# Attention mixers of a two-block decoder: the grouped heads are projected before the neighbourhood heads

## The chip, the cores and the metric

The kernel runs on one core of a Trainium2 chip, as one program. The time is in device microseconds (us), and the medians below are over several executions. One execution was also taken by the hardware profiler, and every row in this document comes from that one.

## What is computed

The first block has two layers. Each layer is a feed-forward net (FFN), four attention mixers side by side, a projection with `w_out`, and a second FFN. Then comes a second block with other mixers, which the change does not touch. There are 256 tokens, in two tiles of 128, and 1024 features. Cut to what matters:

```python
h = rms_norm(x, mix_norm[l])
pa, pb, pc, pd = jnp.split(h @ w_in[l], IN_SPLITS, axis=-1)
ya = neighbourhood_mixer(pa, ...)   # q, k normed per head; logits + bias table
yb = mla_mixer(pb, ...)             # "latent": two more projections, rotary
yc = diff_mixer(pc, ...)            # "differential": difference of two softmaxes
yd = gqa_mixer(pd, ...)             # "grouped": q, k normed, axial rotary, no bias
x = x + jnp.concatenate([ya, yb, yc, yd], axis=-1) @ w_out[l]
x = x + 0.5 * swiglu(rms_norm(x, ffn2_norm[l]), ...)
```

Each mixer has four heads of 64 and gives 256 columns, so that each owns two of the eight row blocks of `w_out` (128 rows each): the neighbourhood heads own blocks 0 and 1, latent 2 and 3, differential 4 and 5, grouped 6 and 7.

## The kernel before

All products run as matmuls of up to 512 columns. A large product takes three of them: operands are split into a high and a low part (`xTh`, `xTl` for the activations, `hi`, `lo` for the weights), and the sum of hi·hi, lo·hi and hi·lo is kept. Weights come from HBM in units of 512 KB into three staging buffers (`st`); ScalarE (ACT) rounds a unit to `hi`, VectorE (DVE) subtracts to get `lo`. Six split buffers lie ahead of TensorE (PE), and a unit is cut when PE is done with the unit six before it.

In each layer `mixers` records the projections as a stream that PE always has work in, and the attention as background generators (`differential`, `latent`, `neighbourhood`, `grouped`) that are resumed between the matmuls of that stream. A small clock model (class `Clock`, fixed costs per operation) says when a generator is due. After that the tile scheduler places the instructions of every engine; each engine then runs its own list strictly in order.

- Projections before the change, in the order of the code: differential q and k (512 columns), latent (416), differential v (256), latent's two small ones, neighbourhood q and k (512, `un`), neighbourhood v (256, `vn`), grouped q, k and v (512, `ug`). The list of weights at the start of `decoder` has the same order.
- One softmax is at work at a time (`att["busy"]`), in `softmax_pv`. A mixer has four jobs (differential eight), and a job covers 128 queries by 256 keys of two heads. A job makes scores into two PSUM buffers (`sps`, one for each half of the job), takes a maximum on DVE (`nm`), exponentials on ACT (`E`), transposes `E` on PE (`tps`), copies it out (`PT`), multiplies with v, and transposes back (`yt`). Then DVE writes `y`. Where the logits have no bias (latent, grouped) the exponential reads `sps` itself, so the buffer is free only after it; with a bias (neighbourhood, differential) DVE reads `sps` and frees it.
- When a mixer's jobs for a token tile are done, `post` norms them (`yn`), PE transposes `yn`, and ACT and DVE write it as `yT`, high and low.
- `neighbourhood` and `differential` keep their transposed q and k in the `xg` buffers (`qkT` in the profile); `latent` and `grouped` share one pair (`qT`, `kT`), so `grouped` waits for `"mla_s"`, latent's last scores.
- `wide` then runs the product with `w_out` over `OUT_ORDER`: four units one by one (blocks 4, 5, 2, 3; for each both token tiles and both halves of 512 columns), then the last four together, half by half. `before(k, t)` holds a matmul back until that mixer's `yT` of that token tile is recorded. The first matmuls of the FFN's gate (`xTh`, `xTl`) follow as soon as a token tile's `x` is normed.

Of the kernel before, what the change touches and what calls it, by code (L numbers as in the profile page):

```python
# [39 lines left out]
FIRST = [1, 1, 2, 2, 2]  # L40
WARM = 6
AHEAD = 14
OUT_ORDER = (4, 5, 2, 3, 0, 1, 6, 7)
IN2 = {"ax": 0, "az": 512, "bq": 1024, "bkv": 1536, "bz": 1792,
       "cq": 2304, "ck": 2816, "cv": 3328, "cz": 3840, "g": 4352}
IN2_ORDER = (("cq", 512), ("ck", 512), ("cv", 512), ("bq", 512), ("bkv", 256),
# [183 lines left out]
def decoder(ctx, tc, a, out):  # L230
# [33 lines left out]
    for l in range(L):  # L264
        for f in (1, 2):
            if f == 2:
                wi = a["w_in"][l]
                ws.add(wi, 8, 512, 2, (OFF_DIFF, OFF_DIFF + 512))
                ws.add(wi, 8, 416, 2, (OFF_MLA, OFF_MLA + 416))
                ws.add(wi, 8, 256, 4, (OFF_DIFF + 512, OFF_DIFF + 768))  # L270
                ws.add(a["mla_w_uq"][l], 2, 384, 2)
                ws.add(a["mla_w_ukv"][l], 1, 512, 1)
                ws.add(wi, 8, 512, 2, (OFF_NA, OFF_NA + 512))
                ws.add(wi, 8, 256, 4, (OFF_NA + 512, OFF_NA + 768))
                ws.add(wi, 8, 512, 2, (OFF_GQA, OFF_GQA + 512))
                for k in OUT_ORDER:
                    ws.add(a["w_out"][l][k * 128:(k + 1) * 128, :], 1, D, 1)
            for c in range(0, DFF, 512):
                n = min(512, DFF - c)
                for w in ("gate", "up"):  # L280
                    first = (l, f, c, w) == (0, 1, 0, "gate")
                    ws.add(a[f"ffn{f}_w_{w}"][l], 8, n, FIRST if first else 1024 // n,
                           (c, c + n))
            ws.add(a[f"ffn{f}_w_down"][l], KF, D, 1)
# [125 lines left out]
    def spawn(gen, first=False, at=None):  # L410
        at = clock.last if at is None else at
        bg.insert(0 if first else len(bg), [gen, at, at])
# [83 lines left out]
    def proj(K, n, per, evac, skew=False):  # L496

        ps = [psM() for _ in range(2)]
        per = per if isinstance(per, list) else [per] * (K // per)
        block = len(per) if skew else 1  # L500
        k0 = 0
        for u0 in range(0, len(per), block):
            w = [get() for _ in range(block)]
            for t in range(2):
                k = k0
                for u in range(block):
                    for j in range(per[u0 + u]):
                        acc([(ps[t][:, :n], 0, n)], xTh[:, k, tok(t)], xTl[:, k, tok(t)],
                            w[u], j, k == 0, k == K - 1)
                        if k < K - 1:  # L510
                            tick()
                        k += 1
                    if t == 1:
                        ws.end(w[u])
                if k == K:
                    done = timed(evac, t, ps[t])
                    tick()
            k0 = k
        return done
# [192 lines left out]
    def mixers(l, cols, rows, nlam, norm_out):  # L712
# [43 lines left out]
        def new_v(nh):  # L756
            return wk.tile([128, 2, nh, 64], F, tag="v", name="v", bufs=3)
# [22 lines left out]
        def ev_u(u):  # L780
            return lambda t, ps: scaled(u[:, t, :], ps, rstd[t])
# [178 lines left out]
        def neighbourhood(u, v):  # L960
            qT, kT = yield from qk_transposed(u, lambda: new_qk(0), "na_q", "na_k",
                                              64 ** -0.5, 64, lambda: "diff_s" in finished)
            yield lambda: (4, 1) in finished
            y = new_y()
            jobs = []
            for t in range(2):
                for p in range(2):
                    jobs.append(dict(
                        t=t, nk=2, bias=[bias[:, t, 4 + 2 * p + s, :] for s in range(2)],
                        qk=[(pair(qT[64 * s:64 * s + 64, :, tok(t)], p),  # L970
                             pair(kT[64 * s:64 * s + 64], p)) for s in range(2)],
                        v=[[v[:, k, 2 * p + s, 0:64] for k in range(2)] for s in range(2)],
                        y=heads(y[:, t, tok(p)])))
            yield from softmax_pv(jobs, post_rms(y, "na_beta", 0),
                                  have_v=lambda: "na_v" in finished)

        def grouped(ug):
# [51 lines left out]
                split_out(kT[:, 0, tok(t)].bitcast(R), kT[:, 2, tok(t)].bitcast(R), p3[:, 2])  # L1029
                yield 0  # L1030
            yield
            yield lambda: (2, 1) in finished
            y = new_y()
            jobs = []
            for t in range(2):
# [17 lines left out]
        proj(8, 256, 4, ev_v(vd))  # L1053
        finished.add("diff_v")
        w += [get(), get()]
        un = wk.tile([128, 2, 512], F, tag="u", name="u")
        vn = new_v(4)
        spawn(neighbourhood(un, vn), at=proj(8, 512, 2, ev_u(un)))
        proj(8, 256, 4, ev_v(vn))
        finished.add("na_v")  # L1060
        ug = []

        def ev_gqa(t, ps):
# [4 lines left out]
            scaled(ug[t], ps, rstd[t])  # L1068
        at = proj(8, 512, 2, ev_gqa)
        spawn(grouped(ug), at=at)  # L1070

        def before(k, t):
            k0 = k // 2 * 2
            return (k0, t) in finished and (k0 == 6 or (k0, 1) in finished)
        wide(OUT_ORDER, yTh, yTl, [1] * 4 + [4], lambda t, h, ps: norm_out.update(t, h, ps, 1.0),
             before)

# [364 lines left out]
```

## Time and profile before

| | us |
|---|---|
| median of 3 runs | 1328.57 (1325.44 to 1332.58) |
| the profiled execution | 1329.33 |
| its span, first to last instruction | 1327.2 |

| engine | busy us | share of the span |
|---|---|---|
| PE matmuls | 1302.8 | 98% |
| PE weight loads | 1049.7 | 79% |
| DVE | 792.8 | 60% |
| ACT | 722.8 | 54% |
| POOL | 27.6 | 2% |

A PE that is shown busy is not PE at its peak, since matmuls are pipelined and their ends are modelled: what counts is from one matmul's start to the next. The mixers of the first layer run from about 202 to 345 us, those of the second from about 728 to 870 us. The profile has a clock that the throttle grants to PE, in tenths of full speed; two levels occur, full (2.4 GHz) and half (1.2 GHz).

### The profile page before, as it was taken

The page shows a single profiled execution, that of the slowest core. Times are in us where ns is not written, and L with a number is a line of the kernel's source. Part 1 is how long each engine was busy: PE and PEld are TensorE (multiplying, and loading weights), DVE is VectorE, ACT ScalarE, POOL GpSimd, SP SyncE. Part 2 cuts the span into 40 slices and gives each one's busy share as a digit, 9 for nine tenths or more (in the row PEclk, how much of TensorE's full clock was granted, in tenths as well). Part 3 has the DMA queues.
Part 4 walks back from the last instruction along what each step waited for, and adds up shares of the span by engine and source line. Part 5 has one row for each costly group of instructions (what it writes and reads, how often), then busy time and mean ns, then how long its engine had stood idle before and what let it go on. Part 6 is the DMA issues. An engine that isn't in the chain of part 4 may idle for free.

```text
span 1327.2 us, 17825 instructions
## 1 busy us (share of the span) xinstructions
PE 1302.8 (98%) x6514; PEld 1049.7 (79%) x6514; DVE 792.8 (60%) x1615; ACT 722.8 (54%) x1223; POOL 27.6 (2%) x44
## 2 busy tenths in 40 slices
PE   9999999999999999999999999999999999999997
PEld 7788888766788888788888876678888787678886
DVE  5655449895655544755545898565554565555475
ACT  6544437865644443644434676664444467566543
POOL 0000001000000000100000000000000000000000
PEclk9999999998999999999999998999999999999999
DMA  8766657432466655666665733156655484245752
GB/s 268 224 183 185 181 165 236 125 96 64 153 191 188 191 175 175 192 189 188 177 188 145 245 112 96 49 174 184 185 182 182 149 264 141 80 142 167 206 167 80
DMA packets 109815, 221.80 MB, mean 167 GB/s; under 512 B 7456, under 2 KB 30368, under 8 KB 109728
## 3 DMA queue, kind: packets, MB, share of 16 engines
q1 hardware_dynamic: 109152, 220.04, 55.5%
q8 instruction: 51, 0.84, 0.3%
q10 hardware_dynamic: 576, 0.63, 0.1%
q14 instruction: 36, 0.29, 0.1%
HBM read 219.59 MB, written 1.05 MB: 166 GB/s over the span
## 4 chain that ended last, share of the span: by engine, by line
PE 82%; DVE 6%; DMA 6%; ACT 4%; issue 1%; POOL 0%; POOLq 0%; ACTq 0%; SPq 0%; DVEq 0%
PE mmps L333 71%; PE tps L337 6%; PE sps L333 3%; PE tps L333 3%; DVE lo L154 2%; DMA st<-in_ffn_w_gate_dram 2%; DMA st<-in_w_in_dram 2%; ACT hi L154 2%; DMA st<-in_ffn_w_up_dram 2%; ACT junk L154 1%; DVE xTl L153 1%; ACT xTh L153 0%; POOL r L154 0%; DVE x L153 0%; ACT E L153 0%
## 5 line engine op out<-in xcount | busy, mean ns | idle before, releaser
L154 DVE TENSOR_TENSOR lo<-st,hi 128x1024 fp32r<-128x1024 f32 (+2 forms) x403 | 488.0, 1214 | 400.5 <-ACT hi L154 399.6
L154 ACT ACTIVATE hi<-st 128x1024 fp32r<-128x1024 f32 (+2 forms) x403 | 421.7, 1050 | 433.6 <-PE mmps L333 353.8
L333 PE MATMUL mmps<-hi,xTh 128*128 128x512 f32 (+2 forms) x1200 | 452.5, 377 | 1.3 <-ACT xTh L153 1.0
L333 PE MATMUL mmps<-hi,xTl 128*128 128x512 f32 (+2 forms) x1200 | 446.5, 372 | 0.0
L333 PE MATMUL mmps<-lo,xTh 128*128 128x512 f32 (+2 forms) x1200 | 446.3, 372 | 0.0
L333 PEld LDWEIGHTS mmps<-hi,xTh 128*128 128x128 f32 x1200 | 226.3, 189 | 43.2 <-issue 2.6
L333 PEld LDWEIGHTS mmps<-hi,xTl 128*128 128x128 f32 x1200 | 226.3, 189 | 37.8 <-issue 0.5
L333 PEld LDWEIGHTS mmps<-lo,xTh 128*128 128x128 f32 x1200 | 226.4, 189 | 36.6 <-issue 1.0
L333 PE MATMUL mmps<-lo,hTh 128*128 128x512 f32 x352 | 140.2, 398 | 0.0
L333 PE MATMUL mmps<-hi,hTh 128*128 128x512 f32 x352 | 139.8, 397 | 0.0
L333 PE MATMUL mmps<-hi,hTl 128*128 128x512 f32 x352 | 115.6, 395 | 0.0
L333 PE MATMUL mmps<-hi,yT 128*128 128x512 f32 (+1 forms) x248 | 89.8, 420 | 0.6 <-ACT yT L153 0.6
L333 PEld LDWEIGHTS mmps<-hi,hTl 128*128 128x128 f32 x352 | 66.2, 188 | 15.6
L333 PEld LDWEIGHTS mmps<-hi,hTh 128*128 128x128 f32 x352 | 66.2, 188 | 15.4
L333 PEld LDWEIGHTS mmps<-lo,hTh 128*128 128x128 f32 x352 | 66.1, 188 | 15.3
L333 PEld LDWEIGHTS mmps<-hi,yT 128*128 128x128 f32 x248 | 46.3, 191 | 12.1 <-issue 2.0
L154 POOL TENSOR_TENSOR r<-ms,mhalf 128x1 f32<-128x1 f32 x40 | 27.4, 688 | 1294.7 <-DVE ms L154 1294.6
L333 PE MATMUL mmps<-lo,yT 128*128 128x512 f32 (+1 forms) x124 | 50.4, 406 | 0.0
L154 ACT ACTIVATE E<-E,nm 128x256 f32<-128x256 f32 (+1 forms) x80 | 38.2, 480 | 14.9 <-DVE nm L154 14.7
L153 ACT ACTIVATE fg<-mmps,r 128x512 f32<-128x512 f32 (+1 forms) x48 | 31.1, 652 | 21.7 <-PE mmps L333 21.7
L153 ACT ACTIVATE xTh<-tps,gains 128x128 fp32r<-128x128 f32 x112 | 31.7, 366 | 16.8 <-PE tps L337 16.8
L153 ACT ACTIVATE PT<-tps 128x512 f32<-128x512 f32 (+1 forms) x56 | 27.9, 502 | 22.0 <-PE tps L337 21.5
(172 smaller groups left out, 1039.3 us busy)
## 6 DMA issues: line engine op xcount, KB each, us to landing
st<-in_w_in_dram SPq DMA_DIRECT2D x90, 512.0 KB, 3.8
st<-in_ffn_w_up_dram SPq DMA_DIRECT2D x88, 512.0 KB, 4.1
st<-in_ffn_w_down_dram SPq DMA_DIRECT2D x88, 512.0 KB, 3.6
st<-in_ffn_w_gate_dram SPq DMA_DIRECT2D x87, 512.0 KB, 3.8
st<-in_w_out_dram SPq DMA_DIRECT2D x24, 512.0 KB, 3.7
st<-in_w_in_dram SPq DMA_DIRECT2D x8, 416.0 KB, 4.2
scratch<-in_t5b_dram SPq DMA_DIRECT2D x4, 512.0 KB, 4.8
scratch<-in_nab_dram SPq DMA_DIRECT2D x4, 512.0 KB, 6.8
```

Of the source, the lines that this page charges most:

```text
L153: return f(*args, **kw)
L154: return f(*args, **kw)
L333: nc.tensor.matmul(ps, lhsT=lhsT, rhs=rhs, start=start, stop=stop)
L337: nc.tensor.transpose(ps, src, ident)
```

## The change

Three things move, and no operation is added or taken away. The grouped projection (one of 512 columns: q, k and v) stands directly behind differential v. Neighbourhood v comes next, and neighbourhood q and k are the last projection, so that this mixer's generator starts last. The list of weights has the same new order. In the softmaxes the grouped mixer now waits for the differential one to be finished, `(4, 1)`, and the neighbourhood mixer for the latent one, `(2, 1)`: they have changed places. `OUT_ORDER` ends with 6, 7, 0, 1, and in `before` the neighbourhood blocks are now those whose second token tile need not be done for the first to go ahead.

```diff
-OUT_ORDER = (4, 5, 2, 3, 0, 1, 6, 7)
+OUT_ORDER = (4, 5, 2, 3, 6, 7, 0, 1)
...
                 ws.add(a["mla_w_ukv"][l], 1, 512, 1)
+                ws.add(wi, 8, 512, 2, (OFF_GQA, OFF_GQA + 512))
+                ws.add(wi, 8, 256, 4, (OFF_NA + 512, OFF_NA + 768))
                 ws.add(wi, 8, 512, 2, (OFF_NA, OFF_NA + 512))
-                ws.add(wi, 8, 256, 4, (OFF_NA + 512, OFF_NA + 768))
-                ws.add(wi, 8, 512, 2, (OFF_GQA, OFF_GQA + 512))
...
         def neighbourhood(u, v):
             qT, kT = yield from qk_transposed(u, lambda: new_qk(0), "na_q", "na_k",
                                               64 ** -0.5, 64, lambda: "diff_s" in finished)
-            yield lambda: (4, 1) in finished
+            yield lambda: (2, 1) in finished
...
                 split_out(kT[:, 0, tok(t)].bitcast(R), kT[:, 2, tok(t)].bitcast(R), p3[:, 2])
                 yield 0
             yield
-            yield lambda: (2, 1) in finished
+            yield lambda: (4, 1) in finished
...
         w += [get(), get()]
-        un = wk.tile([128, 2, 512], F, tag="u", name="u")
-        vn = new_v(4)
-        spawn(neighbourhood(un, vn), at=proj(8, 512, 2, ev_u(un)))
-        proj(8, 256, 4, ev_v(vn))
-        finished.add("na_v")
         ug = []
...
         at = proj(8, 512, 2, ev_gqa)
         spawn(grouped(ug), at=at)
+        un = wk.tile([128, 2, 512], F, tag="u", name="u")
+        vn = new_v(4)
+        proj(8, 256, 4, ev_v(vn))
+        finished.add("na_v")
+        spawn(neighbourhood(un, vn), at=proj(8, 512, 2, ev_u(un)))
 
         def before(k, t):
             k0 = k // 2 * 2
-            return (k0, t) in finished and (k0 == 6 or (k0, 1) in finished)
+            return (k0, t) in finished and (k0 == 0 or (k0, 1) in finished)
```

The lists of the engines are the same up to the projection of neighbourhood v. From there on they differ, in both layers in the same way. Three places follow.

The first is PE in the first layer, where latent's first scores (`sps<-kT,qT`) stand. `u` is the neighbourhood's q and k, `yn` the differential mixer's second token tile, and `mmps<-...,yT` the product with `w_out`. Before:

```order
L337 MATMUL tps_2763<-ident_106,u_2081 128x128 x4
L337 MATMUL tps_2789<-ident_106,u_2081 128x128 x4
L333 MATMUL sps_2798<-kT_2684,qT_2683 128x256
L333 MATMUL sps_2799<-kT_2684,qT_2683 128x256
L333 MATMUL mmps_2758<-hi_2591,yT_1716 128x512
L333 MATMUL sps_2855<-kT_2684,qT_2683 128x256
L337 MATMUL tps_2868<-ident_106,E_2800 128x128 x2
L333 MATMUL sps_2856<-kT_2684,qT_2683 128x256
L337 MATMUL tps_2868<-ident_106,E_2800 128x128 x2
L333 MATMUL sps_2930<-kT_2684,qT_2683 128x256
L333 MATMUL sps_2931<-kT_2684,qT_2683 128x256
L337 MATMUL tps_2905<-ident_106,yn_2853 128x128 x2
```

After:

```order
L333 MATMUL sps_2781<-kT_2654,qT_2653 128x256
L333 MATMUL sps_2782<-kT_2654,qT_2653 128x256
L333 MATMUL mmps_2824<-hi_2570,yT_1716 128x512
L333 MATMUL mmps_2823<-hi_2630,yT_1716 128x512
L333 MATMUL mmps_2823<-lo_2631,yT_1716 128x512
L333 MATMUL mmps_2824<-hi_2630,yT_1716 128x512
L333 MATMUL mmps_2824<-lo_2631,yT_1716 128x512
L333 MATMUL mmps_2823<-hi_2630,yT_1716 128x512
L333 MATMUL mmps_2824<-hi_2630,yT_1716 128x512
L333 MATMUL sps_2845<-kT_2654,qT_2653 128x256
L333 MATMUL sps_2846<-kT_2654,qT_2653 128x256
L333 MATMUL sps_2872<-kT_2654,qT_2653 128x256
```

The eight transposes of `u` are gone from here, seven matmuls of `w_out` stand between the first job's scores and the second's, and the scores of the second job and half of the third now stand in one piece; `yn` follows that piece.

The second is DVE between the same `y` and `yn`, its last twelve rows. Before (`hss`, `ms`, `r`, `q` are the steps of a reciprocal square root, here of the grouped heads and of `y`):

```order
L153 TENSOR_REDUCE nm<-sps 128x1
L154 SCALAR_TENSOR_TENSOR r<-q,r 128x4
L154 TENSOR_SCALAR r<-ms 128x6
L154 TENSOR_REDUCE hss<-scratch 128x6
L154 SCALAR_TENSOR_TENSOR q<-ms,r 128x4
L153 TENSOR_REDUCE nm<-sps 128x1
L154 TENSOR_TENSOR q<-q,r 128x4
L154 TENSOR_SCALAR ms<-hss 128x6
L154 SCALAR_TENSOR_TENSOR r<-q,r 128x4
L154 TENSOR_SCALAR r<-ms 128x6
L154 SCALAR_TENSOR_TENSOR q<-ms,r 128x6
L154 TENSOR_TENSOR yn<-y,r 128x256
```

After:

```order
L154 TENSOR_TENSOR q<-q,r 128x4
L154 TENSOR_TENSOR pr<-ug,prt 128x128
L154 SCALAR_TENSOR_TENSOR r<-q,r 128x4
L154 TENSOR_TENSOR lo<-st,hi 128x1024
L154 SCALAR_TENSOR_TENSOR q<-ms,r 128x4
L154 RECIPROCAL rs<-sm 128x2
L154 TENSOR_TENSOR lo<-st,hi 128x1024
L154 TENSOR_TENSOR q<-q,r 128x4
L153 TENSOR_REDUCE nm<-sps 128x1
L154 SCALAR_TENSOR_TENSOR r<-q,r 128x4
L153 TENSOR_REDUCE nm<-sps 128x1
L154 TENSOR_TENSOR yn<-y,r 128x256
```

The end of the grouped heads' rotary (`pr`) and two cuts of weights (`lo`) have come in ahead of `yn` and ahead of the second job's maxima.

The third is PE at the scores of the grouped mixer, its second to fourth job. Before:

```order
L333 MATMUL sps<-kT,qT 128x256 x3
L337 MATMUL tps<-ident,E 128x128 x2
L333 MATMUL mmps<-lo,yT 128x512
L333 MATMUL mmps<-hi,yT 128x512 x2
L333 MATMUL mmps<-lo,yT 128x512
L333 MATMUL mmps<-hi,yT 128x512 x2
L333 MATMUL sps<-kT,qT 128x256 x6
L337 MATMUL tps<-ident,yn 128x128 x2
L333 MATMUL tps<-PT,ug 64x128 x4
L333 MATMUL mmps<-lo,yT 128x512
L333 MATMUL sps<-kT,qT 128x256 x6
```

After:

```order
L333 MATMUL sps<-kT,qT 128x256 x3
L337 MATMUL tps<-ident,E 128x128
L333 MATMUL sps<-kT,qT 128x256 x3
L337 MATMUL tps<-ident,E 128x128 x3
L337 MATMUL tps<-ident,u 128x128 x4
L333 MATMUL sps<-kT,qT 128x256 x6
L337 MATMUL tps<-ident,u 128x128 x4
L333 MATMUL sps<-kT,qT 128x256 x5
```

The matmuls of `w_out` between these jobs are gone; the eight transposes of `u` have come here.

## Rows read from the trace of the kernel before

**Rows 1.** Busy time by stage: stretch, us, then PE, PEld, DVE, ACT, POOL; clock, DMA.

```profile
279.00:302.00 23.00, 20.45 (x115) 14.31 (x114) 20.24 (x96) 13.96 (x39) 0.55 (x1) 0.89 0.21 64
...
319.00:345.00 26.00, 24.65 (x153) 17.29 (x154) 15.19 (x42) 16.21 (x50) 2.48 (x5) 1.00 0.36 113
360.00:380.00 20.00, 19.91 (x92) 16.13 (x91) 12.23 (x12) 9.63 (x12) 0.00 (x0) 1.00 0.71 213
...
805.00:828.00 23.00, 20.58 (x112) 14.53 (x110) 19.48 (x95) 13.60 (x38) 0.55 (x1) 0.85 0.19 56
```

**Rows 2.** Waits of PE, 279 to 345 us: total us, times, longest.

```profile
PE sps L333 <- ACT E L153: 2.3, 4, 1.1
PE tps L337 <- ACT E L153: 0.5, 1, 0.5
PE mmps L333 <- ACT xTh L153: 0.5, 1, 0.5
```

**Rows 3.** The stretches at half clock, columns as in rows 1.

```profile
286.70:290.05 3.35, 3.28 (x11) 2.80 (x12) 2.35 (x14) 1.51 (x6) 0.00 (x0) 0.50 0.00 0
...
300.40:307.10 6.70, 6.70 (x23) 4.65 (x23) 4.05 (x17) 2.48 (x10) 0.55 (x1) 0.50 0.49 151
812.40:819.10 6.70, 6.25 (x23) 4.62 (x24) 5.13 (x32) 3.58 (x13) 0.00 (x0) 0.50 0.00 0
```

**Rows 4.** PE in order of time (start, us; in brackets the idle time before).

```profile
279.88 0.27 PE L337 MATMUL tps<-ident,yt 128*128 128x128 f32 x1
...
280.90 1.12 PE L337 MATMUL tps<-ident,u 128*128 128x128 f32 x8
...
281.86 1.03 PE L333 MATMUL sps<-kT,qT 96*128 96x256 f32 x4
...
283.58 0.70 PE L333 MATMUL sps<-kT,qT 96*128 96x256 f32 x2 [0.47 <-ACT E L153]
...
286.77 2.07 PE L333 MATMUL sps<-kT,qT 96*128 96x256 f32 x4 [1.14 <-ACT E L153]
288.64 0.63 PE L337 MATMUL tps<-ident,yn 128*128 128x128 f32 x2
```

**Rows 5.** DVE in order of time: `y` and `yn` of that token tile.

```profile
280.19 0.48 DVE L153 TENSOR_SCALAR y<-tps,rs 128x64 f32<-128x64 f32 x2 [0.92 <-PE tps L337]
...
286.92 0.42 DVE L154 TENSOR_TENSOR yn<-y,r 128x256 f32<-128x256 f32 x1
```

**Rows 6.** DVE by shape, 279 to 302 us: count, busy us, mean ns, idle before.

```profile
L154 DVE TENSOR_TENSOR lo<-st,hi 128x1024 fp32r<-128x1024 f32 x3 | 3.7, 1220 | 0.9 <-ACT hi L154 0.9
...
L154 DVE TENSOR_TENSOR prt<-ug,scratch 128x64 f32<-128x64 f32 x8 | 1.5, 218 | 0.0
...
L153 DVE SCALAR_TENSOR_TENSOR qkT<-tps,qcol,qkT 128x256 fp32r<-128x256 f32 x2 | 1.0, 480 | 0.0
L154 DVE TENSOR_TENSOR q<-q,r 128x6 f32<-128x6 f32 x6 | 1.0, 158 | 0.0
```

**Rows 7.** From a mixer's `y` (DVE) to its transposed `yn` (PE), latent's second tile.

```profile
317.02 0.29 DVE L153 TENSOR_TENSOR y<-tps,rs 128x128 f32<-128x128 f32 x1 [0.59 <-PE tps L337]
...
320.77 0.38 PE L337 MATMUL tps<-ident,yn 128*128 128x128 f32 x2
```

**Rows 8.** PE at the grouped mixer's first, second and third job.

```profile
320.05 0.62 PE L333 MATMUL sps<-kT,qT 64*128 64x256 f32 x5
...
321.67 0.61 PE L333 MATMUL sps<-kT,qT 64*128 64x256 f32 x3 [0.51 <-ACT E L153]
...
325.11 0.89 PE L333 MATMUL sps<-kT,qT 64*128 64x256 f32 x6
```

**Rows 9.** ACT: single operations that stand between exponentials, and the FFN's first `xTh`.

```profile
281.54 0.47 ACT L153 ACTIVATE qkT<-tps,qcol 128x256 fp32r<-128x256 f32 x1 [0.36 <-PE tps L337]
...
285.67 0.60 ACT L153 ACTIVATE PT<-tps 128x512 f32<-128x512 f32 x1
...
340.20 1.12 ACT L153 ACTIVATE xTh<-tps,gains 128x128 fp32r<-128x128 f32 x4
```

## The prediction

> **What bounds the kernel now.** I read the busy times first. PE is busy for 98% of the span by the page's first part, so no other engine limits the whole; what can change is the time in which PE stands still or runs slowly. The busy times by stage show where that is [rows 1]. In the FFN PE has no idle time to speak of: 92 matmuls in 20 us, or 0.22 us from one start to the next. Between 279 and 302 us, where latent's and the neighbourhood's softmax run, 2.55 of 23 us are idle and the granted clock is 0.89; the second layer shows the same (805 to 828 us, 2.4 us idle, clock 0.85). The waits of PE say what it stood still for [rows 2]: 2.3 us for exponentials that free a score buffer, 0.5 us for the transposes of `E`, 0.5 us for the FFN's first `xTh`; together 3.3 us in the mixers' second half, the same again in the second layer. The windows at half clock are the other loss [rows 3]: 3.35 and 6.70 us in the first layer, 6.70 us in the second. There the same four score matmuls take 2.07 us that took 1.03 us before [rows 4]. At half speed a stretch costs at most half its length, so 16.75 / 2 = 8.4 us in both layers together. All that a new order of these instructions can win is therefore about 6.6 + 8.4 = 15 us, or 1.1%. DVE is the engine to watch in the same stage: 20.24 of 23 us busy [rows 1].
>
> **What doesn't change.** The matmuls, cuts of weights, exponentials and DMAs are the same in number and shape. The projections moved past each other have units of the same 512 KB, used up by PE at nearly the same rate: 12 matmuls of 512 columns are 12 x 0.22 = 2.6 us. Cuts run up to six units ahead, so that a cut that comes a few us later on DVE still lands before its use. SP's list moves by one weight load, and POOL's not at all. The evacuation of the grouped projection now comes right after latent's statistics; these have read the shared buffer long before, since the code takes them at the start of `latent`. I cost all this at nothing; six units are the cover.
>
> **Step A, latent's first scores.** The eight transposes of `u` (0.96 us from their start to the scores' start [rows 4]) and some `w_out` matmuls now stand behind these scores, so that PE comes to them about 2 us earlier. That is no gain by itself, since DVE is late next. From `y` to `yn` DVE took 6.73 us before [rows 5], and PE went from `yt` at 279.88 us to `yn` at 288.64 us, 8.76 us, with 1.6 us of waits among the rows and some 2 us of it at half clock [rows 3, 4]. In the new list of DVE two `lo` of 1.22 us each and eight small rotary products (0.2 us) with four sums come in ahead of `yn`; four splits of `qkT` (0.48 us), two reductions and some steps of 0.16 us leave [rows 6]. In means that is about 5.4 us more and 3.7 us less; as neighbours overlap by some 0.08 us, I take 1.3 us more, 8 us in all. PE then has between `yt` and `yn`: 15 large matmuls (3.3 us), four transposes (0.4 us), and five halves of score jobs at 0.5 us (2.6 us), 6.3 us. DVE's 8 us and 0.7 us at both ends make 8.7 us. So PE stands still for about 2.4 us, where before it lost 1.6 us of waits and 1 us of half clock. I take 0 for the step; its ends are -0.5 us (the rotary slips behind) and +1 us (the third job's half waits as well for the second's exponential).
>
> **Step B, the hand-over to the second mixer.** Before, the neighbourhood's q and k lay ready in buffers of their own. Now the grouped heads come second, and their `qT`, `kT` are latent's: the transposes can only start when latent's scores have been read, and ACT and DVE split them out before a grouped score runs. In the new list six such transposes stand behind latent's last `E`, with six matmuls and one transpose (1.4 us) between the last of them and the first score. The splits take two ACT and two DVE operations of at most 0.48 us in sequence [rows 6, 9], so 1 to 2 us: 0 to 0.6 us of wait. Besides, `yn` of latent's first token tile now has only 2.4 us of PE work between itself and its `yt`, while from `y` to that transpose it takes 3.75 us [rows 7]: 1.1 to 1.4 us. The waits of before at this place were 0.5 us [rows 2]. I take +0.8 us; the ends are 0 (DVE is less loaded here without the rotary) and +2.
>
> **Step C, the grouped scores.** A score buffer is free again after maximum and exponential: from the first job's scores to the second's, 1.62 us with a wait of 0.51 us [rows 8]. Before, six `w_out` matmuls stood between the second and the third job, and none waited. Now there are four transposes of `E` and four of `u` (0.9 us), between the third and the fourth only four of `u`. At the same time the splits of `u` go onto ACT (0.47 us each) beside `PT` (0.60 us) [rows 9], ahead of the exponentials for which PE waits. The two jobs then wait 1.62 - 0.35 - 0.9 = 0.4 us and 1.62 - 0.35 - 0.4 = 0.9 us, and up to 1 us more each if a `PT` and a split lie in between; the wait of 0.51 us at the second job goes, as four matmuls now stand there. I take +1.0 us, ends -0.5 and +2.5.
>
> **Step D, the end of the mixers.** The neighbourhood is last now, and 19 matmuls of the FFN's gate stand ahead of the last six-matmul groups of `w_out`, which wait for its `yn`. They cover that chain, but their `xTh` (1.12 us for four [rows 9], eight of them) and weight cuts of about 1 us lie in ACT's list ahead of the last `yT`. The wait for `xTh` before was 0.5 us [rows 2]. I take +0.4 us, ends -0.5 and +2.
>
> **Clock.** PE falls behind at the same place as before (A), so I leave the half-clock stretches as they are: 0. The ends are -8.4 us (none is left) and +6.7 us (one more of 6.7 us in each layer).
>
> **Sum.** 0 + 0.8 + 1.0 + 0.4 = 2.2 us a layer, 4.4 us for two. On the profiled execution's 1329.33 us that is 1333.7 us; that execution lies 0.8 us above the median of the three, so 1333 us.
>
> **Rivals.**
> 1. *PE never runs short, and the half clock goes.* Latent's scores start earlier and have seven `w_out` matmuls (1.5 us) between the first two jobs, which is what the exponential needs. Then A to D come to nothing and the 8.4 us come back: 1328.6 - 8.4 = 1320 us. For it speaks that the half clock sets in right where PE stood still for 1.14 us [rows 4], and that the same mixer hand-over led to a second fall in one layer only, so that little decides. Against it speaks DVE's list, with two `lo` ahead of the second job's maxima.
>    The Trainium skill says something stronger (Trainium Kernel Development and Optimization, section Performance Expectations): matmul busy time is a bad measure of how near a kernel is to its limit, and the share of weight loading is a good one. By that share, 62% (14.31 of 23 us) against the FFN's 81% (16.13 of 20) [rows 1], this stage alone would have 4.2 us of slack in place of the 2.55 us idle that the row shows; won in both layers, that is again some 1320 us. The small transposes and score matmuls of this stage load weights in another ratio, so I hold to the idle time.
> 2. *Slower: the grouped scores and the neighbourhood's preparation block each other.* They share ACT and DVE only in the new order. If `PT` and a split stand ahead of the exponential in both late jobs (C at +2.5), B is at +2, and the longer stand brings one more half-clock stretch in each layer (3.4 us each at half loss), the sum is 2 x (2 + 2.5 + 0.4) less A's 0, or 9.8, less what the two share (the same waits at half clock, some 3), plus 6.7: 13.5 us, 1342 us. It decides from the point at which PE stands still for over 1 us more than once in the grouped scores.
> 3. *The change moves nothing*, since every list is filled with the same work and PE is busy for 98%: 1328.6 us. This is within 0.5% as my forecast is.
>
> **How the numbers follow.** A measurement of this kernel tells about 0.5% (6.6 us) from no change. Forecast and third rival lie within 1322 and 1335 us: 0.55, of which the forecast has 0.35. Rival 1 has 0.17 and rival 2 has 0.28; the second is the likelier, since each of the steps B, C and D adds a wait. For 8 in 10 the range runs from rival 1's 1320 to 1343 us, just over rival 2.
>
> **What would show it.** Right: `yn` of the differential mixer's second tile waits on DVE or the scores ahead of it wait for over 2 us (A); a wait of the grouped scores or of latent's `yn` at the hand-over (B); two waits of grouped scores for exponentials, about 1 us each (C); the `yT` wait at the end under 1 us (D); half clock in each layer's stage of latent's scores. Wrong: no half clock in either layer, PE idle under 2 us a layer there, or a wait for `lo`, `hi` or a DMA in the projections.

## The result and the profile after

| | median, us | lowest to highest | executions |
|---|---|---|---|
| before | 1325.76 | 1324.14 to 1332.58 | 9 |
| after | 1334.77 | 1330.24 to 1342.37 | 9 |

The ratio is 1.0068, with an interval of 1.0051 to 1.0086: the change makes the kernel slower by just over the 0.5% that the measurement can tell. A second set of six executions (e11 below) gave 1.0065 (1.0041 to 1.0090). The profiled execution of after took 1342.37 us, the longest of its nine.

One sum helps to read all that follows. Each execution reports its span and the mean clock that PE was granted. Span times clock is about the time that it would have taken at full clock, since PE is busy for 98% of it; the rest of the span is about what half clock cost. That rest counts every half-clock stretch of an execution, those outside the mixers too, and takes a wait within a stretch for lost work (1.5 us in the first stretch shown below), so it is a little too large. Means with their standard errors:

| | executions | at full clock, us | lost by half clock, us |
|---|---|---|---|
| before | 90 | 1317.1 ± 0.2 | 7.8 ± 0.3 |
| after | 15 | 1321.7 ± 0.3 | 11.9 ± 1.0 |
| difference | | +4.6 | +4.1 |

So about half of the loss is waits and instruction order, and about half is the clock.

The waits of PE in the first layer's mixers, 279 to 360 us, in after (total us, times, longest):

```profile
PE sps L333 <- ACT E L153: 3.8, 4, 2.4
PE sps L333 <- DVE mx L153: 0.9, 1, 0.9
PE mmps L333 <- ACT yT L153: 0.6, 2, 0.5
PE tps L337 <- ACT PT L153: 0.5, 1, 0.5
PE tps L337 <- ACT yt L153: 0.4, 1, 0.4
PE tps L333 <- DVE y L153: 0.2, 1, 0.2
PE tps L333 <- ACT PT L153: 0.2, 1, 0.2
```

They sum to 6.6 us, against 3.3 us in [rows 2] and 0.3 us for a `yT` that stands there too. PE in order of time shows where they lie. First latent's scores:

```profile
283.96 1.15 PE L333 MATMUL sps<-kT,qT 96*128 96x256 f32 x4 [0.57 <-ACT E L153]
287.52 1.22 PE L333 MATMUL sps<-kT,qT 96*128 96x256 f32 x2 [2.41 <-ACT E L153]
...
300.28 0.55 PE L337 MATMUL tps<-ident,pr 128*128 128x128 f32 x3 [0.53 <-ACT PT L153]
301.06 0.67 PE L333 MATMUL tps<-PT,v 128*64 128x128 f32 x8 [0.23 <-DVE y L153]
302.18 0.44 PE L337 MATMUL tps<-ident,yn 128*128 128x128 f32 x2 [0.45 <-ACT yt L153]
303.09 0.79 PE L333 MATMUL mmps<-hi,yT 128*128 128x512 f32 x1 [0.47 <-ACT yT L153]
...
313.34 0.62 PE L333 MATMUL sps<-kT,qT 64*128 64x256 f32 x3 [0.32 <-ACT E L153]
314.43 0.50 PE L333 MATMUL sps<-kT,qT 64*128 64x256 f32 x2 [0.47 <-ACT E L153]
...
325.78 0.38 PE L333 MATMUL sps<-qkT 64*128 64x256 f32 x1 [0.94 <-DVE mx L153]
```

The first two rows are latent's second and third job (0.57 and 2.41 us, in place of the 0.47, 0.20 and 1.14 us around [rows 4]). The next four are the hand-over from latent to grouped, where PE goes from one small operation to the next and waits before each: 1.7 us, with a wait of 0.17 us for `PT` just before them 1.85 us. Then come grouped's late jobs (0.32 and 0.47 us) and the neighbourhood's scores (0.94 us). Why the third job waits so long is read from DVE in the same 4 us:

```profile
283.97 1.22 DVE L154 TENSOR_TENSOR lo<-st,hi 128x1024 fp32r<-128x1024 f32 x1
...
285.25 1.21 DVE L154 TENSOR_TENSOR lo<-st,hi 128x1024 fp32r<-128x1024 f32 x1
...
286.45 0.42 DVE L153 TENSOR_REDUCE nm<-sps 128x1 f32<-128x256 f32 x1
...
287.19 0.42 DVE L154 TENSOR_TENSOR yn<-y,r 128x256 f32<-128x256 f32 x1
```

The second job's scores are there at about 285 us; its maximum runs at 286.45, behind two cuts of weights.

The stretches at half clock in the mixers (columns as in [rows 1]; the clock is the last number but two):

```profile
286.05:292.85 6.80, 5.33 (x16) 4.34 (x16) 5.10 (x22) 3.52 (x11) 0.00 (x0) 0.50 0.53 155
303.10:306.50 3.40, 3.40 (x10) 2.81 (x11) 1.52 (x6) 1.05 (x4) 0.15 (x1) 0.50 0.11 43
316.70:320.10 3.40, 3.40 (x14) 2.45 (x10) 0.46 (x2) 1.78 (x6) 0.00 (x0) 0.51 0.00 0
821.90:825.30 3.40, 3.40 (x11) 2.49 (x9) 2.76 (x16) 2.28 (x7) 0.00 (x0) 0.50 0.37 132
835.60:839.00 3.40, 3.40 (x11) 2.61 (x11) 1.50 (x6) 1.05 (x4) 0.35 (x1) 0.50 0.06 23
849.20:852.60 3.40, 3.40 (x12) 2.46 (x14) 0.46 (x2) 1.80 (x7) 0.00 (x0) 0.50 0.00 0
```

Each layer has three: behind latent's scores, behind the hand-over, and behind grouped's scores. Before had two in the first layer, the second of them (from 300.4 us) at its own hand-over from latent to the neighbourhood, and one in the second [rows 3]. A further stretch (760.5 to 767.3 us) lies in work that the change doesn't touch.

### The profile page after: what moved, and what is told of

It reads as the page before. It is cut to its first block, busy times and chain, and to the rows that moved or that the text cites. A ratio compares the mean times of both kernels' runs of the same rounds, so it can differ in the third digit from the quotient of the medians.

```text
span 1340.5 us, 17839 instructions
## 1 busy us (share of the span) xinstructions
PE 1308.4 (98%) x6514; PEld 1053.2 (79%) x6514; DVE 794.6 (59%) x1615; ACT 725.5 (54%) x1225; POOL 26.2 (2%) x44
## 4 chain that ended last, share of the span: by engine, by line
PE 84%; DMA 5%; DVE 5%; ACT 3%; issue 1%; POOL 0%; POOLq 0%; ACTq 0%; DVEq 0%; SPq 0%
PE mmps L333 73%; PE tps L337 6%; DMA st<-in_w_in_dram 3%; PE sps L333 3%; PE tps L333 3%; DVE lo L154 2%; ACT hi L154 1%; DMA st<-in_ffn_w_up_dram 1%; ACT junk L154 1%; DMA x<-in_x_dram 0%; DVE xTl L153 0%; DVE x L153 0%; DMA st<-in_ffn_w_gate_dram 0%; DVE q L154 0%; POOL r L154 0%
## 5 line engine op out<-in xcount | busy, mean ns | idle before, releaser
L333 PE MATMUL mmps<-hi,yT 128*128 128x512 f32 (+1 forms) x248 | 93.7, 435 | 1.3 <-ACT yT L153 1.3
L333 PEld LDWEIGHTS mmps<-hi,yT 128*128 128x128 f32 x248 | 49.4, 201 | 13.8 <-ACT yT L153 3.6
L333 PE MATMUL sps<-kT,qT 64*128 64x256 f32 (+2 forms) x144 | 31.8, 375 | 7.6 <-ACT E L153 7.6
```

The lines of the kernel that those rows point to most:

```text
L333: nc.tensor.matmul(ps, lhsT=lhsT, rhs=rhs, start=start, stop=stop)
```

## The experiments

**Do the spread and the loss hold?** e1 is the kernel before once more, e11 the changed one.

> The kernel before, once more, to see how its executions spread and what clock each was granted. In the changed kernel the nine executions run from 1330 to 1342 us with mean clocks of 0.996 to 0.987; if the half-speed part is taken out (span times clock) all nine lie between 1320.2 and 1323.1 us, where the one profiled execution of before gives 1327.2 x 0.992 = 1316.6 us. Theory 1 (waits cost about 5 us, the rest is clock): the executions of before all give 1316 to 1318 us with the half-speed part taken out, and their mean clocks are 0.993 to 0.997. Rival (before and after have the same waits and differ by clock alone): span times clock also gives 1320 to 1323 us for most executions of before.

Measured: 1325.98 us, ratio 0.9997 (0.9979 to 1.0014); at full clock 1317.7 us on average of twelve, lost 7.1 us. Single executions lie between 1315.2 and 1320.2 us at full clock, wider than theory 1 said.

> The changed kernel once more, to see whether its larger loss by half clock (12.2 us on average of nine executions against 8 us in some 60 of before) holds, and at which places another execution of the same instructions shows it. Theory C: loss 11 to 13 us on average, full-clock time 1321 to 1322 us, median 1333 to 1337 us, ratio 1.005 to 1.009; in the trace stretches at half clock behind latent's scores, behind the hand-over to grouped or behind grouped's scores, not all of them in each layer. Rival (the nine were a draw): loss 8 us, 1330 us, ratio 1.003.

Measured: 1335.97 us; at full clock 1322.1, lost 11.6 us. Theory 1 and theory C (formed below, from e2) hold in size: the difference is partly waits (always there) and partly clock (more of it on average). The trace of e11 shows that the clock is a draw in a single execution. Its waits are the same to a tenth, with 2.4 us at latent's third job in both layers, yet its first layer keeps full clock throughout, and the second has one stretch:

```profile
279.00:302.00 23.00, 18.16 (x110) 12.81 (x111) 20.30 (x80) 14.36 (x38) 0.55 (x1) 1.00 0.39 115
302.00:324.00 22.00, 20.09 (x129) 13.75 (x128) 12.81 (x38) 13.08 (x40) 1.09 (x2) 1.00 0.11 28
812.20:815.60 3.40, 3.40 (x12) 2.91 (x11) 2.16 (x8) 2.39 (x7) 0.00 (x0) 0.50 0.51 168
```

So a list of instructions sets how much is lost to the clock on average, not where the clock falls in one execution; only means over executions compare.

**Are the two cuts what latent's third job waits for?** e2 holds cuts back between latent's first and second scores.

```diff
-        if ws.can_cut():
+        if ws.can_cut() and not att.get("hold"):
...
+                att["hold"] = jobs[0].get("hold") == i1      # latent's jobs have hold=1
```

> The changed kernel, in which no weight cut is recorded between latent's first scores and its second, so that the two cuts (1.22 us each on DVE) fall behind the second job's maxima. Theory 1 (these two cuts are what the third job's scores wait for): the wait of 2.41 us falls to 0.7 us or less in both layers, 3.4 us in all, and the half clock right behind it (6.8 and 3.4 us) goes or gets shorter, up to 5 us: 1326 to 1331 us, ratio to before 1.000 to 1.004. Rival (the loss sits in the scores of grouped and neighbourhood): the waits there stay and the time stays at 1333 to 1336 us, ratio 1.0055 to 1.008. Second rival (half clock comes by itself, not behind waits): the wait goes, 3.4 us are gained, the stretches at half clock stay in number and length: 1331 us.

Measured: 1349.99 us, ratio 1.0152 (1.0116 to 1.0187). At full clock 1321.7 ± 1.1 us, as the change itself; lost by half clock 23.8 ± 3.5 us. The wait went as theory 1 said, from 2.41 to 0.71 us, so the cuts were its cause. But PE's waits between 279 and 360 us still sum to over 6 us: others came up at the hand-over (1.2 us for `yt`, 0.8 us for `kT`) and at `yT` (1.4 us). And the clock became worse, which none of the three had. The two stretches at half clock of its trace, and the end of the first:

```profile
300.15:324.03 23.88, 23.86 (x87) 16.36 (x88) 8.66 (x25) 9.34 (x30) 1.10 (x2) 0.50 0.06 21
321.18:324.03 2.85, 2.85 (x9) 2.27 (x8) 1.24 (x3) 1.15 (x3) 0.00 (x0) 0.50 0.00 0
839.50:859.90 20.40, 20.40 (x75) 14.01 (x74) 6.90 (x22) 8.68 (x29) 0.55 (x1) 0.50 0.00 0
```

PE is busy for 23.86 of 23.88 us and stays at half clock. What it runs there are score matmuls and transposes, grouped by operation up to 321 us:

```profile
L333 PE MATMUL sps<-kT,qT 64*128 64x256 f32 x24 | 8.4, 489 | 0.8 <-ACT kT L153 0.8
L337 PE MATMUL tps<-ident,E 128*128 128x128 f32 x12 | 3.2, 425 | 0.0
L333 PE MATMUL mmps<-hi,yT 128*128 128x512 f32 x4 | 3.2, 794 | 0.0
...
L333 PE MATMUL mmps<-lo,yT 128*128 128x512 f32 x2 | 1.4, 702 | 0.0
```

In 21 us there are six matmuls of 512 columns. Full clock comes back at 324 us, behind seven of them among nine operations. The Trainium skill (TensorE: Matmul & The Clock Gate, section What's actually happening) says that the gate goes by how busy PE has been lately and that half rate is the idle state. As to the fall the trace agrees, since the first stretch begins at 300.1 us behind two waits of PE:

```profile
298.38 0.55 PE L337 MATMUL tps<-ident,pr 128*128 128x128 f32 x3 [1.22 <-ACT yt L153]
...
300.17 0.58 PE L333 MATMUL sps<-kT,qT 64*128 64x256 f32 x1 [0.77 <-ACT kT L153]
```

As to the way back it does not: PE is shown busy for 24 us and does not get full clock back. This gave theory C: PE loses its clock wherever it has run small matmuls alone for a while, whether it stands still or not, and gets it back behind a row of large ones. It was a guess from two stretches; what the traces say to it stands behind e10.

**Are grouped's late jobs slowed by the neighbourhood's splits?** e3 makes `u`'s transposes wait for grouped's last scores.

```diff
-    64 ** -0.5, 64, lambda: "diff_s" in finished)
+    64 ** -0.5, 64, lambda: "gqa_s" in finished)   # set by grouped's last scores
```

> The changed kernel, in which the neighbourhood's transposes of u wait until the grouped mixer's last scores are recorded, so that its splits on ACT and DVE no longer stand among grouped's exponentials. Theory 1 (these splits cost 0.4 to 1 us a layer in grouped's scores and a similar wait in the neighbourhood's own): the two waits of grouped's third and fourth job (0.32 and 0.475 us) go or halve, the neighbourhood's scores come about 2 us later, and the time moves by -2 to +2 us: 1332 to 1337 us, ratio 1.005 to 1.0085. Rival (mutual blocking of grouped and neighbourhood is the main loss): 1326 to 1329 us, ratio 1.000 to 1.0025, with the half clock behind grouped's scores gone.

Measured: 1339.09 us, ratio 1.0079 (1.0051 to 1.0106); at full clock 1326.9 ± 0.4, lost 8.9 ± 1.6. So it is 5 us longer at full clock than the change, most of it in waits (8.8 us in 279 to 360 us, where the change has 6.6): those in grouped's scores went, but PE's waits for `yt` (1.5 us a layer, 0.4 in the change), `PT` (1.9 and 0.7) and `yT` (0.8 and 0.6) grew, where the mixers now follow each other with less beside them. Mutual blocking was not the main loss; starting the preparation early is the better of the two.

**Which half of the change does it?** e4 has the projections and weights of before with the new order of softmaxes and `w_out`; e7 the new projections with the old order of softmaxes (grouped then waits for `"na_s"`, the neighbourhood's last scores).

```diff
--- e4, on before: only these lines of the change, and the same in `before(k, t)`
-OUT_ORDER = (4, 5, 2, 3, 0, 1, 6, 7)
+OUT_ORDER = (4, 5, 2, 3, 6, 7, 0, 1)
-            yield lambda: (4, 1) in finished     # neighbourhood
+            yield lambda: (2, 1) in finished
-            yield lambda: (2, 1) in finished     # grouped
+            yield lambda: (4, 1) in finished
--- e7, on after: these lines as before, and in grouped
-            yield lambda: (4, 1) in finished
+            yield lambda: "na_s" in finished and (2, 1) in finished
```

> One part of the change alone: projections and weights in the order of before, softmaxes and w_out's rows in the new order (grouped second to last, neighbourhood last). Theory 1 (half of the loss comes from latent's scores, where the moved projections leave the two cuts; the other half from the new order of the softmaxes): latent's scores wait 1.8 us as before, grouped's and the neighbourhood's wait about 2 us a layer: 1329 to 1332 us, ratio 1.0025 to 1.005. If the order of the projections is the whole cost: 1326 us, ratio 1.000. If the order of the softmaxes is the whole cost: 1334 to 1336 us, ratio 1.007.

> The other part of the change alone: projections and weights in the new order, but the neighbourhood's softmax second to last and grouped's last (grouped waits for the neighbourhood's last scores), and the rows of w_out in the old order. The softmax order alone gave +4.2 us of full-clock time and no more half clock (loss 8.1 us). If the two parts add up, this one gives little full-clock time (1317 to 1319 us) and all of the extra half clock (loss 11 to 13 us): 1330 to 1333 us, ratio 1.0025 to 1.005. If the extra half clock needs both: loss 8 us and 1326 to 1329 us, ratio 1.000 to 1.002.

| | at full clock | lost | median | ratio |
|---|---|---|---|---|
| e4, softmaxes alone | 1321.1 ± 0.4 | 8.1 ± 0.6 | 1330.96 | 1.0024 (1.0009 to 1.0039) |
| e7, projections alone | 1319.7 ± 1.2 | 29.7 ± 3.1 | 1349.01 | 1.0191 (1.0157 to 1.0224) |
| both | 1321.7 ± 0.3 | 11.9 ± 1.0 | 1334.77 | 1.0068 (1.0051 to 1.0086) |

For e4 the time came out as theory 1 said, but all of it at full clock. The extra half clock comes with the projections, and more of it without the new softmax order than with it: the parts don't add up, and 29.7 us was beyond anything I expected. The trace of e7 shows it as one long stretch in the second layer:

```profile
845.60:872.90 27.30, 27.04 (x117) 17.93 (x117) 8.44 (x35) 13.50 (x46) 0.73 (x2) 0.50 0.10 29
```

Of these 117 operations, five are matmuls of 512 columns. PE's idle time is 0.3 us. It is e2's picture again. What e4's 4.0 us at full clock consist of stays partly open: its waits between 279 and 360 us sum to 4.0 us, only 0.4 above before.

**Does the clock follow PE's standstill or the lack of large matmuls?** Six kernels add matmuls of 512 columns by a matrix of zeros into a running sum, so that they stream and change nothing. A tiny POOL operation makes the zero from a value of an earlier job and so sets from when they can run.

```diff
+            def fill(n, e):
+                xz = xTh[:, 0:2, :].rearrange("p k n -> p (k n)")
+                nc.gpsimd.tensor_scalar(zR, e, 0.0, None, op0=ALU.mult)
+                for _ in range(n):
+                    nc.tensor.matmul(pss[0][0], lhsT=zR.to_broadcast([128, 128]), rhs=xz,
+                                     start=False, stop=False)
```

e5 fills latent's long wait alone, e6 grouped's late jobs alone, e8 latent's wait in the kernel before.

> The changed kernel with eight extra matmuls of 512 columns (by a stationary matrix of zeros, so that they add nothing to the sum they go into) in each layer between the second and the third job of latent's scores, where PE stands still for 2.41 us; three or four matmuls of w_out move into the same place. Measure: span times clock is the time with the half-speed part taken out (1321.5 us on average in the nine executions of the change, 1317.0 in 35 of before), span less that is the loss by half clock (12.2 and 8.1 us). Theory A (the half clock follows PE's standstill): the stretches that begin about 1 us behind it (6.8 and 3.4 us) go, the loss falls to 7 to 9 us, the full-clock time stays at 1320 to 1321.5: 1329 to 1331 us, ratio to before 1.0015 to 1.003. Theory B (it follows the share of small matmuls in the stage, or comes by chance): loss 11 to 13 us as in the change, 1333 to 1335 us, ratio 1.005 to 1.007.

> The changed kernel with three such extra matmuls of 512 columns ahead of the third and of the fourth job of grouped's scores, six in each layer (1.3 us at 0.22 us), where it waits 0.32 and 0.475 us and has no matmul of w_out. Full-clock time: up by 0.4 to 0.9 us a layer, 1322.5 to 1323.5 us. Theory A (half clock follows the long standstill of latent's scores alone): the loss stays at 11 to 13 us: 1336 to 1338 us, ratio 1.007 to 1.009. Theory B (it follows stages with small matmuls alone): the stretch of 3.4 us behind grouped's scores goes in each layer, the loss falls by 3.4 to some 9 us: 1333 to 1335 us, ratio 1.005 to 1.0065.

> The kernel before with four extra matmuls of 512 columns (zeros) in each layer between the second and third job of latent's scores, where PE stood still for 1.14 us. Theory A: the half clock that begins there goes in most executions, the loss falls from 8.1 to 4 to 5 us, full-clock time 1317 to 1318: 1322 to 1324 us, ratio 0.9965 to 0.998. Theory B: loss as before, 8 us, 1326 to 1328 us, ratio 1.000 to 1.0015.

| | at full clock | lost | median | ratio |
|---|---|---|---|---|
| e5 | 1321.7 ± 0.5 | 10.3 ± 1.5 | 1333.84 | 1.0051 (1.0026 to 1.0076) |
| e6 | 1324.2 ± 0.6 | 10.7 ± 2.0 | 1337.60 | 1.0081 (1.0050 to 1.0113) |
| e8 | 1317.7 ± 0.5 | 10.2 ± 1.1 | 1329.35 | 1.0035 (1.0017 to 1.0052) |

None separates: in e5 and e6, with one of three places filled, the loss is within its error of 11.9 us. By the times e5 and e8 speak against theory A and e6 for it, but none was a clean test, since the fillers did not land in the waits. In e5 PE still stands 1.3 us for an exponential and 0.7 us for the zero at latent's scores, in e6 0.7 us at grouped's third job, and in e8 waits for exponentials of 1.9 us (latent's scores) and 1.4 us (the hand-over) stand in place of 1.14 and 0.55 us.

e9 fills all three places of the change with 21 matmuls a layer; e12 has 16. e10 fills two places of before. `fs` counts the fillers ahead of a job's scores, `fv` those ahead of its product with v, for jobs 0 to 3:

```diff
+    latent   e9:  fs=(0, 0, 8, 0), fv=(0, 0, 2, 5)    grouped  e9:  fs=(0, 0, 3, 3)
+    latent   e12: fs=(0, 0, 8, 0), fv=(0, 0, 0, 4)    grouped  e12: fs=(0, 0, 2, 2)
+    latent   e10: fs=(0, 0, 6, 0), fv=(0, 0, 1, 3)
```

> The changed kernel with extra matmuls of 512 columns (zeros, they add nothing) at the three places of each layer behind which its trace shows half clock: eight at latent's third job, seven around latent's last values, six ahead of grouped's third and fourth job; 21 a layer, or 4.5 us at 0.22 us. At these places PE stands still for 2.4, 1.7 and 0.95 us, which can take up most of them: full-clock time 1321 to 1326 us. Theory C (PE loses its clock wherever it has run for a few us with small matmuls only, standing still or not, and gets it back behind a row of large ones): the loss by half clock falls from 12.2 to 2 to 6 us: 1326 to 1332 us, ratio to before 1.000 to 1.005. Rival (the half clock has another cause or comes by chance): loss 10 to 13 us, 1334 to 1340 us, ratio 1.006 to 1.010.

> As the kernel with extra matmuls at three places, with 16 of them in each layer instead of 21: eight at latent's third job as there, four instead of seven around latent's last values, four instead of six ahead of grouped's third and fourth job. Five fewer are 1.1 us a layer, 2.2 us for two, as far as they don't lie in waits. Theory C with room to spare: the loss by half clock stays at 2 to 3 us, full-clock time falls from 1323.8 to 1321.5 to 1323: 1325.5 to 1327 us, ratio to before 0.998 to 1.000, so that it comes out level with before or just ahead of it. If the fillers are needed in this number: stretches come back behind grouped's scores or the hand-over, loss 5 to 9 us: 1329 to 1332 us, ratio 1.002 to 1.004.

> The kernel before with extra matmuls of 512 columns at the two places of each layer behind which its trace shows half clock: six at latent's scores, four around latent's last values; ten a layer, 2.2 us, of which the waits there (1.8 and 0.7 us) can take up most. Full-clock time 1317 to 1319 us. Theory C: the loss falls from 8 to 2 to 4 us: 1321 to 1325 us, ratio 0.996 to 0.9995. Rival: loss 8 us as before, 1327 to 1329 us, ratio 1.0005 to 1.002.

| | at full clock | lost | median | ratio |
|---|---|---|---|---|
| e9, 21 a layer | 1323.8 ± 0.4 | 1.8 ± 0.2 | 1327.19 | 1.0000 (0.9985 to 1.0015) |
| e12, 16 a layer | 1322.3 ± 0.4 | 4.4 ± 0.7 | 1328.74 | 1.0021 (1.0007 to 1.0036) |
| e10, before with 10 a layer | 1324.1 ± 0.9 | 15.0 ± 2.1 | 1341.91 | 1.0107 (1.0075 to 1.0138) |

e9 shows that the extra half clock of the changed kernel comes from these three places and not by chance. With 42 matmuls more, none of use, it is some 8 us faster than the change and level with before; in none of its twelve executions is more than 2.7 us lost, and what remains includes the few us at the kernel's very end that all show. Its trace has full clock in both layers' mixers:

```profile
279.00:302.00 23.00, 20.98 (x124) 14.69 (x123) 19.64 (x75) 13.14 (x39) 1.79 (x5) 1.00 0.30 94
302.00:324.00 22.00, 21.19 (x138) 14.28 (x136) 12.98 (x43) 14.30 (x44) 1.55 (x4) 1.00 0.18 49
...
828.00:856.00 28.00, 27.47 (x188) 18.87 (x188) 15.02 (x55) 18.92 (x59) 1.88 (x4) 1.00 0.14 39
```

The fillers mostly run where PE stood, here at latent's scores, where waits of 0.99 us (for the zero from POOL) and 0.16 us are left of 0.57 and 2.41 us:

```profile
281.15 0.96 PE L531 MATMUL mmps<-xTh,zR 128*128 128x512 f32 x3 [0.99 <-POOL zR L529]
...
282.63 1.51 PE L531 MATMUL mmps<-xTh,zR 128*128 128x512 f32 x5
...
285.00 0.70 PE L333 MATMUL sps<-kT,qT 96*128 96x256 f32 x2 [0.16 <-ACT E L153]
```

With five fewer (e12), 1.5 us come back at full clock and 2.6 us more are lost by half clock, so fewer fillers did not pay. Whether these 2.6 us lie in the mixers isn't shown: e12's one trace has full clock in both layers' mixers, and a stretch near the kernel's start, at 11.1 to 14.5 us. In e10 theory C's expectation failed. At full clock it is 7 us longer: its waits between 279 and 360 us sum to 5.0 us against 3.6, and the fillers' 2.2 us come on top, (1.4 + 2.2) x 2 = 7.2 us. The fillers stand behind the waits instead of in them (1.9 us for an exponential at latent's scores, 1.6 us at the hand-over), and the clock loss almost doubled. Whether before can be cured in the same way is open. No version beat before.

**Standstill or lack of large matmuls: what the traces say.** e9 took both away at once: large matmuls came in, and PE's waits between 279 and 360 us fell from 6.6 to 2.8 us. So it does not tell which of the two brings the clock down, and theory C does not hold as a rule. Of the three places only grouped's scores lost large matmuls by the change. At the hand-over PE goes from one of them to the next in less time than before; the first two rows are before, the third is the change, whose next one starts at 303.09 us (above):

```profile
295.31 0.62 PE L333 MATMUL mmps<-hi,yT 128*128 128x512 f32 x2
302.78 0.79 PE L333 MATMUL mmps<-hi,yT 128*128 128x512 f32 x1
...
297.63 0.48 PE L333 MATMUL mmps<-hi,yT 128*128 128x512 f32 x1
```

What grew there is the waits, from 0.55 to 1.85 us. Nor do small matmuls and transposes alone always bring or keep half clock. The first row is e4, the other two are e7's first layer; none of the three stretches has a matmul of 512 columns:

```profile
845.80:852.20 6.40, 6.24 (x46) 4.01 (x45) 4.68 (x19) 4.82 (x16) 0.55 (x1) 1.00 0.31 86
...
316.50:323.30 6.80, 6.54 (x32) 4.25 (x31) 2.38 (x13) 3.80 (x14) 0.00 (x0) 0.50 0.36 110
323.40:330.70 7.30, 7.30 (x55) 4.88 (x54) 3.88 (x13) 6.07 (x21) 0.55 (x1) 1.00 0.00 1
```

In e4 the clock stays full, and in e7 it comes back with no large matmul near. The fall goes with standstill in every trace: all half-clock stretches of the mixers, in all 14 traces, begin in waits of PE or shortly behind them (0.7 us or more in all). In e2, where latent's wait was shortened without adding large matmuls, the trace has no half clock behind latent's scores in either layer. But that is one execution, in which other waits came up, and the same waits don't always bring half clock (e11's first layer). So the cause of the fall stays open.

## Why the prediction was right and where it was not

1333 us against 1334.8 us measured, in the range; but this flatters it. The median of before that I started from (1328.6 us, of three) came to 1325.8 us with nine, so that the forecast difference was 4.4 us and the measured one about 9. The case "within 0.5%" was given 0.55 and did not occur: with 0.68% the time lies just on the slower side, which had 0.28.

- **The sum of the waits: right, partly by luck.** Forecast 4.4 us, at full clock measured 4.6 us. The terms in the first layer, as waits of PE, before and after:
  - A, latent's scores: I said that PE would stand for about 2.4 us between `yt` and `yn`, because of the two cuts on DVE. It stands for 0.57 and 2.41 us, and e2 shows the cuts to be the cause of the longer wait. But PE waits at the scores, for an exponential behind the late maxima, and not for `yn` itself, from which I had worked the number out (from `y` to `yn` DVE took 8.7 us, not 8), so that the agreement of 2.4 with 2.41 is in part luck. And I set 1 us of half clock of before against it. As waits the step is 1.8 to 3.0 us, or +1.2, not 0.
  - B, hand-over: +0.8 forecast, from 0.55 to 1.85 us measured, +1.3. `yn`'s transpose waits as I said, but for 0.45 us (put down to the `yt` that was done last) where I took 1.1 to 1.4; the chain `PT`, `y`, `yt`, `yT` waits at each link.
  - C, grouped's scores: +1.0 forecast, 0.5 to 0.95 us measured, +0.4. The waits are at the two jobs named, 0.32 and 0.47 us where I took 0.4 and 0.9; the other 0.16 us are for a `yT` right behind them.
  - D, end of the mixers: +0.4 forecast; the waits of before there (0.5 us for `xTh`, 0.3 us for `yT`) went, so -0.8. What I did not see is the neighbourhood's own scores, +0.9, which wait for the maximum on DVE that frees their buffer.
  
  Together +3.0 us a layer, 6 us for two, somewhat more than the 4.6 us at full clock; where the rest is covered I can't place. That the waits are the 4.6 us is argued from their size and not shown: e4 is 4.0 us longer at full clock with only 0.4 us a layer more of waits.
- **Clock: the step that failed.** I left it at 0, since PE falls behind at the same place as before. It does so there, but the waits at A, B and C all grew, and the trace of the change has half clock behind the hand-over in both layers, where before had it in one [rows 3], and behind grouped's scores, where before had none. At grouped's scores the matmuls of `w_out` are gone as well; in C I had even noted that they go, and costed the wait alone. Measured +4.1 us, which e9 takes away. Which of the two brings the clock down, the waits or the lack of large matmuls, stays open.
- **Rival 2** had the right kind of end, one more half-clock stretch a layer, by another way: its point of decision (PE standing still for over 1 us more than once in grouped's scores) was not reached, and the clock fell all the same. Its 13.5 us were too many.
- **Rival 1** fell: PE ran short at all of A, B and C. The share of weight loading, by which the Trainium skill (Trainium Kernel Development and Optimization, section Performance Expectations) would read the slack, in 279 to 302 us went from 62% [rows 1] to 59% (13.61 of 23.00 us):

```profile
279.00:302.00 23.00, 18.82 (x101) 13.61 (x100) 18.33 (x73) 13.27 (x35) 0.55 (x1) 0.85 0.34 95
```

  In e9 it is 64% with work of no use, so here it told how full PE was, and not what could be won.

## What to carry to other kernels

When an order of instructions is changed, don't only add up the waits. In a stage of short operations a few waits can be followed by a stretch at half clock, which in e7 lasted 27 us with PE busy throughout; here the clock was about half of the loss. Look also at where the large matmuls go: those added at the waits gave the clock back in one kernel (e9), and those that missed the waits made another slower (e10). Split measured times into span times clock and the rest, over several executions, before explaining a difference of a few us; a single trace shows one draw. When a wait was removed on its own (e2, e3), others came up a few us later.

## What the runs showed of the hardware

PE at 1.2 GHz stayed there for 24 us (e2) and 27 us (e7) with idle time of 0.02 and 0.3 us. In e2 it ran small matmuls with six large ones among them in the first 21 us, and returned to 2.4 GHz behind seven large ones; in e7's first layer it returned after 6.8 us of small ones alone, and kept 2.4 GHz through 7.3 us more of them. Matmuls by zeros, five in 1.51 us, went with 2.4 GHz throughout in e9; in e10 three of them and eight of `w_out` lay in a stretch of 13.6 us at 1.2 GHz. The same instructions in two executions of the change lost 4.0 and 17.4 us by half clock.
